# Room for the sixth head's output gates, and another order of loads and splits, in a decoder layer on one core

## The chip, the core and the metric

The kernel runs on one core of a Trainium2 chip. The core has five engines that work side by side, each through its own queue in order: TensorE (PE in the profile), VectorE (DVE), ScalarE (ACT), GpSimd (POOL) and SyncE (SP), which here issues most of the transfers (DMAs) between device memory and the core's memory (SBUF). Matmuls write to PSUM, a small memory of its own. The metric is device time in microseconds (us) for one launch; less is better.

## The reference, cut to what matters

One layer of a hybrid decoder: 1024 tokens of a prompt and 8 single tokens of samples, 1032 columns in all, 1024 channels, float32.

```python
h = _rmsnorm(x, lp['norm1_w']) * (1 + sc1) + sh1
qkv, gdn_gate, beta_raw, a_raw, sq, sk, sv, ga, gb = _split_in(h @ lp['w_in'])
...
def step(S, inp):
    u_n, w_n, a_n, qd_n, kd_n, last_n = inp
    v_new = u_n - jnp.einsum('bhck,bhkv->bhcv', w_n, S)
    o = jnp.einsum('bhck,bhkv->bhcv', qd_n, S) + jnp.einsum('bhij,bhjv->bhiv', a_n, v_new)
    S = S * last_n[..., None, None] + jnp.einsum('bhck,bhcv->bhkv', kd_n, v_new)
    return S, o
y_a = _gdn_out(o_a, gdn_gate, lp['gdn_onorm_w']) @ lp['w_gdn_out']
y_b = o_b @ lp['w_swa_out']
mix = (jax.nn.sigmoid(ga) * y_a + jax.nn.sigmoid(gb) * y_b) @ lp['w_o']
x = x + gt1 * mix
...
```

Here `step` runs over chunks of tokens, for 8 heads with a state S of 128 x 128 each; `_gdn_out` norms its output and multiplies with silu of the output gate; o_b is the output of a sliding-window attention with sinks. A gated FFN with a short convolution and a last norm follow. The samples use the same weights, but a recurrence of one step from a stored state (state_gdn_S), 512 KB for each head.

## The kernel before

Every large product is made three times in a rounded float format: a weight and an activation are each split into a high part (the rounded value, made by ScalarE, L129) and a low part (the rest, by VectorE, L130), and high x high, high x low and low x high are added in PSUM (`mm3`, L200 to L202). Columns come in three parts of 384, 384 and 264 (0, 1, 2; part 2 holds the samples). A weight column block of 128 is loaded by SP as `raw` (512 KB, L150) and split into `wh` and `wl`.

The stages are: conditioning, norm and attention (to about 400 us), the delta rule (to about 1116 us), the two branches' output projections (to about 1260 us), and then the output projection and the FFN.

In the delta stage a loop runs over heads 0 to 7. For each head h it weaves several streams into one order by priorities; the scheduler that lays out the engines' queues decides the rest. The streams are:

- `unit_inverse(h)`: the inverse of a triangular matrix for each of eight chunks of 128 tokens, by blocks of 16, 32 and 64. On PE its steps are L1065, L1071 (16 to 32), L1083, L1088 (32 to 64) and L1097, L1101 (64 to 128), each with copies by ScalarE and VectorE before the next; some blocks are rearranged by transfers (ud, MR, wd, T). The result is W.
- `delta_scan(h)`: a serial chain over eight chunks. For each chunk: L971 (K times the state S), y on VectorE (L972), L974 (W times y), s on ScalarE (L976), L978 (times kd), and the new S on VectorE (L990); L981 and L982 add the output o, which is later normed (osq, L996), transposed and multiplied with the head's output gates sg (L1010, in place), and stored to oa (L1015).
- `delta_prepare(h+1)`: transposes of K, Q and V of the next head (L210) and its products K K and K Q (L926, L927).
- fillers: the projections from w_in. For head h+2 the convolution inputs; the output gates of head h (`delta_gate`), 1032 columns into the tile sg, which exists once, so that the next head's gates are written only when the last ones are stored; the branch gates ga and gb, written to device memory (sga, sgb); and in the loop's last two rounds `early_out`.

`early_out` projects part 2 (and for two column blocks part 0) of the attention's output ob with w_swa_out, multiplies with gate tiles gt loaded from sgb, and stores to device memory. During scans 6 and 7 its products are paced (`spaced`): six matmuls for each link of the scan. Scan 7 also keeps its small operations (`self.small`), and the multiplications by gates are put behind the small operations that go before them (`passed`). At the seventh column block (i == 6) it issues the loads of six of the eight sample states.

`branches` finishes the projection of ob, computes the samples' one step (`sample_delta`: among its last operations are, for each head, a broadcast load of dlr, eight scalings on ScalarE, `scaled[h]`, an update of the state on VectorE and its store), and projects oa with w_gdn_out, in pairs of column blocks. `order(later, first)` makes the instructions of one list stand behind those of another in the queue of their engine, without a wait between engines. `issue_after` puts an instruction behind a given one in the order. Constants live in three pools: those of the whole run, and cp2, which stays open until after the branches.

Of the kernel before, what the change touches and what calls it, by code (L numbers as in the profile page):

```python
# [18 lines left out]
P = 128  # L19
NP = 1024  # L20
NS = 8
NT = NP + NS
KC = 8
H = 8
# [5 lines left out]
EARLY = (3, 4)  # L30
# [2 lines left out]
QUARTERS = [(0, 256), (256, 256), (512, 260), (772, 260)]  # L33
HALF = [(0, 512), (512, 520)]
QW = 260
KEPT = {"ident", "ones", "mhalf", "phalf", "vecs", "fcw", "mT", "a2"}
COL_GATE, COL_BETA, COL_SQ = 3072, 4096, 4112
COL_SK, COL_SV, COL_GA, COL_GB = 5136, 5392, 5648, 6672
# [26 lines left out]
class Step:  # L65
# [28 lines left out]
        return pool.tile(shape, dt, tag=tag, name=f"{tag}_{self.n}", **kw)  # L94

    def const(self, shape, name, dt=F32):
        pool = self.cp if name in KEPT else self.cp2
        return pool.tile(shape, dt, tag=name, name=name)


# [769 lines left out]
    def delta_gate(self, pa, pool, h):  # L870

        nc = self.nc
        sg = self.t(pool, [P, NT], "sg", bufs=1) if h + 1 < H else self.t(self.pz, [P, NT + 3], "z")[:, :NT]

        def gate_out(t, ps):
            lo, n = PARTS[t]
            th = self.t(pa, [P, 512], "th", bufs=2)[:, :n]
            nc.scalar.activation(th, ps, AF.Tanh, scale=0.5)
            nc.vector.scalar_tensor_tensor(sg[:, lo:lo + n], th, 1.0, ps, op0=ALU.add, op1=ALU.mult)

        self.project(self.win(COL_GATE + h * P), self.h, gate_out)
        nc.gpsimd.tensor_copy(self.sgs[:, h, :], sg[:, NP:NT])
        self.sg[h] = sg
        yield
# [263 lines left out]
    def sample_delta(self, pool2):  # L1148

        nc, I = self.nc, self.I  # L1150
# [18 lines left out]
        c, db = (self.flat_room(self.b1, "b1", x, 2) for x in "hl")  # L1169
# [50 lines left out]
        dlr = self.t(self.dr, [H, NS, P], "dlr")  # L1220
# [16 lines left out]
        for h in range(H):  # L1237
            if h % 4 == 0:
                yield
            d = db[:, h % 2 * NP:h % 2 * NP + NP].rearrange("p (b v) -> p b v", b=NS)  # L1240
            nc.sync.dma_start(d, dlr[h].unsqueeze(0).broadcast_to([P, NS, P]))
            for b in range(NS):
                made = nc.scalar.activation(d[:, b, :], d[:, b, :], AF.Copy, scale=kq[:, h, b, 0:1])
                self.scaled.setdefault(h, []).append(made)
                nc.vector.scalar_tensor_tensor(S0[h][:, b, :], S0[h][:, b, :], self.egb[:, b, 0, h:h + 1], d[:, b, :],
                                               op0=ALU.mult, op1=ALU.add)
            nc.gpsimd.dma_start(self.O[3][0][:, h].rearrange("b k v -> k b v"), S0[h])
# [84 lines left out]
    def early_out(self):  # L1332

        nc = self.nc
# [6 lines left out]
        for i, j in enumerate(EARLY_ORDER):  # L1341
            if i == 3:
                self.obX = {0: self.load_part(self.b1, self.ob, 0, "b1")}
                X.update(self.obX)
            now, w = w, load(EARLY_ORDER[i + 1]) if i < 7 else None
            if i == 6:
                with self.tc.issue_after(self.w_load.ins):
                    for h in range(6):
                        self.load_state(h, states[h // 3])
            for t in (2, 0) if j in EARLY else (2,):  # L1350
                lo, n = PARTS[t]
                s = self.t(self.gt[0], [P, 384], self.gt[1])[:, :n]
                nc.sync.dma_start(s, self.sgb[j][:, lo:lo + n])

                def out(t, ps):
                    with self.passed():
                        nc.vector.tensor_tensor(s, ps, s, op=ALU.mult)
                    nc.gpsimd.dma_start(self.ubd[t][j], s)

                for _ in self.project_steps(now, X, out, (t,), self.fill_psum):  # L1360
                    yield

    def branches(self, pool, pool2):
# [2 lines left out]
        ob = {**self.obX, 1: self.load_part(pool2, self.ob, 1)}  # L1366
        ub = [self.t(pool, [P, KC, n], f"t{t}", bufs=1) for t, (_, n) in enumerate(PARTS)]
        samples, rows, self.scaled = self.sample_delta(pool2), self.last_rows(), {}
        gate = lambda src, j, t: self.gate_part(pool if src is self.sga and j > 5 else self.gt[0], src[j][:, PARTS[t][0]:PARTS[t][0] + PARTS[t][1]], t)

        def yb_out(t, ps):
# [41 lines left out]
        for j0 in (0, 2, 4, 6):  # L1413
            w = []
            for j in (j0, j0 + 1):
                w.append(self.load_w(I["w_gdn_out"][0][:, j * P:(j + 1) * P]))
                for h in {1: range(3, H), 2: (6, 7)}.get(j, ()):
                    self.order(self.scaled[h], self.rounded)
            if 0 < j0 < 6:
                for j in (j0, j0 + 1):  # L1420
                    self.project(w[j - j0], oa, ya_out)
                continue
# [583 lines left out]

    def run(self):
        S, nc = ExitStack, self.nc
        self.constants()
        with S() as ca:  # L2010
            with S() as c:
                pool, psum = self.pool("p2", 1, ctx=c), self.pool("q2", 1, PSUM, ctx=c)
                for tag, bufs in dict(qst=8, raw=2, kh=2, kl=2, E=3, obt=2, pp=2, pc=2, o=2).items():
                    self.bufs[id(pool), tag] = bufs
# [112 lines left out]
```

## Time and profile before

| what | value |
|---|---|
| median of 3 runs (lowest, highest) | 2075.91 us (2066.82, 2076.16) |
| the profiled execution | 2069.76 us |
| its span | 2068.1 us |
| mean granted clock of PE | 0.990 |
| PE busy in 0 to 400 us | 375.15 us, mean clock 1.00 |
| PE busy in 400 to 1116 us | 698.20 us, mean clock 0.98 |
| PE busy in 1116 to 1260 us | 140.88 us, mean clock 0.99 |
| PE busy in 1260 to 2068 us | 795.00 us, mean clock 0.99 |

The last four rows are from the view that sums each engine's busy time in given stretches. The span is the time from the first to the last instruction of one execution. Granted clock is the share of the full TensorE clock that the chip's throttle gave. A row of a timeline has the start, the duration, the engine, the line, the operation, output and input, how often, and in brackets how long the engine stood idle before it and whom it waited for. The chain of waits goes back from the last instruction to what released it at each step.

### The profile page before, as it was taken

How to read it: one execution, taken by the hardware profiler on the slowest of the kernel's cores; microseconds unless marked ns; L12 is line 12 of the kernel's file. 1: busy time of each engine (PE TensorE's matmuls, PEld its weight loads, DVE VectorE, ACT ScalarE, POOL GpSimd, SP SyncE). 2: the span in 40 equal slices, each digit the busy share in tenths (PEclk: the TensorE clock that was granted, in tenths of full speed). 3: DMA queues.
4: the chain of work that ended last, by engine and by line, in shares of the span. 5: the costliest groups of instructions: out<-in, count | busy, mean ns of one | idle time of the engine just before them, and what ended most of it. 6: DMA issues, size and time to landing. Idle time of an engine off the chain costs nothing.

```text
span 2068.1 us, 41309 instructions
## 1 busy us (share of the span) xinstructions
PE 2009.2 (97%) x16245; PEld 1909.6 (92%) x16245; DVE 1356.6 (66%) x2714; ACT 901.7 (44%) x2233; POOL 525.0 (25%) x604
## 2 busy tenths in 40 slices
PE   7999998999999999989999999999999999999998
PEld 4987877799999999989989999999999999999998
DVE  5755767483655746646554575579876777679876
ACT  4664545443344343442442352345544444445444
POOL 2000000121321211201112010104556556543551
PEclk9999999999999999989999999999999999999999
DMA  9256443332322322312248774522333333377783
GB/s 303 62 145 211 137 168 117 100 98 63 83 82 57 78 70 52 92 37 61 64 144 243 233 242 115 174 67 89 98 98 100 111 93 93 124 277 279 265 281 129
DMA packets 300960, 275.75 MB, mean 133 GB/s; under 512 B 59731, under 2 KB 246832, under 8 KB 300749
## 3 DMA queue, kind: packets, MB, share of 16 engines
q1 hardware_dynamic: 294202, 250.66, 39.7%
q0 software_dynamic: 6064, 21.85, 3.0%
q8 instruction: 127, 2.08, 0.4%
q14 instruction: 69, 0.56, 0.1%
q10 hardware_dynamic: 498, 0.61, 0.1%
HBM read 212.93 MB, written 62.51 MB: 133 GB/s over the span
## 4 chain that ended last, share of the span: by engine, by line
PE 85%; DVE 6%; DMA 4%; ACT 3%; issue 1%; SPq 0%; POOL 0%; ACTq 0%; DVEq 0%; POOLq 0%
PE mm L200 19%; PE mm L201 18%; PE mm L202 18%; PE wv L200 3%; PE wv L202 3%; PE wv L201 3%; PE wy L202 2%; PE wy L200 2%; PE wy L201 2%; PE pv L672 1%; DMA raw<-in_w_swa_out_dram 1%; PE pt L210 1%; PE tp L210 1%; PE mm L284 1%; PE rc L978 1%
## 5 line engine op out<-in xcount | busy, mean ns | idle before, releaser
L200 PE MATMUL mm<-b1h,wh 128*128 128x384 f32 (+1 forms) x1520 | 498.1, 329 | 3.4 <-ACT gt L1322 1.6
L201 PE MATMUL mm<-b1l,wh 128*128 128x384 f32 (+1 forms) x1520 | 489.9, 323 | 0.0
L202 PE MATMUL mm<-b1h,wl 128*128 128x384 f32 (+1 forms) x1520 | 488.6, 324 | 0.0
L200 PEld LDWEIGHTS mm<-b1h,wh 128*128 128x128 f32 x1520 | 287.6, 189 | 12.0 <-issue 4.6
L201 PEld LDWEIGHTS mm<-b1l,wh 128*128 128x128 f32 x1520 | 287.6, 189 | 4.4 <-issue 3.1
L202 PEld LDWEIGHTS mm<-b1h,wl 128*128 128x128 f32 x1520 | 286.6, 189 | 3.7 <-issue 2.8
L130 DVE TENSOR_TENSOR wl<-raw,wh 128x1024 fp32r<-128x1024 f32 x82 | 102.6, 1252 | 65.9 <-ACT wh L129 63.7
L129 ACT ACTIVATE wh<-raw 128x1024 fp32r<-128x1024 f32 x83 | 87.1, 1049 | 131.1 <-PE mm L201 80.0
L201 PE MATMUL mm<-pk,w 128*128 128x260 f32 (+1 forms) x440 | 124.7, 284 | 1.1 <-DVE pk L130 1.1
L200 PE MATMUL mm<-pk,w 128*128 128x260 f32 (+1 forms) x440 | 124.7, 284 | 0.0
L202 PE MATMUL mm<-pk,w 128*128 128x260 f32 (+1 forms) x440 | 124.5, 283 | 0.0
L130 DVE TENSOR_TENSOR w<-ws,w 128x512 fp32r<-128x512 f32 x88 | 78.8, 896 | 38.9 <-ACT w L129 38.7
L1666 ACT COPY bml<-mm 128x256 f32<-128x256 f32 (+1 forms) x132 | 49.0, 371 | 102.0 <-PE mm L202 99.4
L200 PE MATMUL mm<-bmh,w 128*128 128x260 f32 (+1 forms) x320 | 90.3, 282 | 0.0
L202 PE MATMUL mm<-bmh,w 128*128 128x260 f32 (+1 forms) x320 | 90.2, 282 | 0.0
L200 PE MATMUL mm<-b2h,wh 128*128 128x384 f32 (+1 forms) x256 | 83.3, 327 | 2.6 <-ACT wh L129 2.6
L1721 DVE SCALAR_TENSOR_TENSOR fa<-fz,fcw,fa 128x512 f32<-128x512 f32 x88 | 73.3, 854 | 18.4 <-ACT fa L1719 18.1
L201 PEld LDWEIGHTS mm<-pk,w 128*128 128x128 f32 x440 | 83.2, 189 | 1.3 <-DVE pk L130 1.3
L201 PE MATMUL mm<-b2l,wh 128*128 128x384 f32 (+1 forms) x256 | 83.6, 327 | 0.0
L200 PEld LDWEIGHTS mm<-pk,w 128*128 128x128 f32 x440 | 83.2, 189 | 0.2 <-ACT bml L1666 0.2
L202 PEld LDWEIGHTS mm<-pk,w 128*128 128x128 f32 x440 | 83.4, 190 | 0.0
L202 PE MATMUL mm<-b2h,wl 128*128 128x384 f32 (+1 forms) x256 | 82.6, 325 | 0.0
(648 smaller groups left out, 5886.7 us busy)
## 6 DMA issues: line engine op xcount, KB each, us to landing
raw<-in_w_in_dram SPq DMA_DIRECT2D x59, 512.0 KB
ws<-in_w_ffn_down_dram SPq DMA_DIRECT2D x55, 256.0 KB
raw<-xd SPq DMA_DIRECT2D x47, 258.0 KB
raw<-in_w_ffn_down_dram SPq DMA_DIRECT2D x47, 256.0 KB
raw<-in_w_ffn_gate_dram SPq DMA_DIRECT2D x22, 512.0 KB
raw<-in_w_ffn_up_dram SPq DMA_DIRECT2D x22, 512.0 KB
qst<-in_w_mod_dram SPq DMA_DIRECT2D x16, 512.0 KB
raw<-in_w_mod_dram SPq DMA_DIRECT2D x16, 512.0 KB
```

Of the source, the lines that this page charges most:

```text
L129: return (self.nc.scalar.activation(hi, x, AF.Copy), (eng or self.nc.vector).tensor_tensor(lo, x, hi.bitcast(F32), op=ALU.subtract))
L130: (eng or self.nc.vector).tensor_tensor(lo, x, hi.bitcast(F32), op=ALU.subtract))
L200: mm(ps, whi, xhi, start=first, stop=False, **kw)
L201: mm(ps, whi, xlo, start=False, stop=False, **kw)
L202: self.last_mm = mm(ps, wlo, xhi, start=False, stop=last, **kw).ins
L210: self.nc.tensor.transpose(out, in_, self.ident[:p, :p])
L284: nc.tensor.matmul(ps[32 * j:32 * j + 32], self.cT[:, k0 + j, :], ws[j // 2][:, j % 2, :], start=k0 == 0, stop=k0 > 0)
L672: nc.tensor.matmul(pv[64 * r:64 * r + 64], V[:, n - back, ch], ps[:, r::2, :], start=back == 0, stop=back == (n > 0))
L978: yield step(nc.tensor.matmul(ds, kd[:, n, :], s, start=True, stop=True))
L1666: self.last_copy = nc.scalar.copy(r[p, i], x[p])
L1721: nc.vector.scalar_tensor_tensor(ai[:, c:e], zi[:, j + c:j + e], col(j), ai[:, c:e], op0=ALU.mult, op1=ALU.add)
```

## The change

It has five parts.

1. Ten constants that only the first stages read (SHORT; 4832 bytes of each partition) move from cp2 to a pool cp1 of the attention's context, which is closed after the attention.
2. A pool `side` of that size is opened then. It holds the output gates of head 5, the sixth (`sg5`). Heads 4 and 6 still share the one tile sg, but head 5's gates wait for neither.
3. In `early_out`, while a paced scan runs, the split of the next w_swa_out weight is ordered behind the last four of the scan's small operations that go before the place reached (only scan 7 keeps them).
4. The six states are loaded behind the last gate tile of the last column block (i == 7), no longer behind the weight at i == 6.
5. In `branches`, the scalings of heads 1 to 7 stand behind the split of the first w_gdn_out weight, those of heads 2 to 7 behind the second's (3 to 7 before), 6 and 7 behind the third's as before; and the broadcasts of dlr for heads 2 and 3 stand behind the load of the second weight, 4 and 5 behind the third's.

```diff
+SHORT = {"triu", "tril", "trilu", "stril", "sink", "qs", "kx", "vx", "zero", "a1"}
 KEPT = {"ident", "ones", "mhalf", "phalf", "vecs", "fcw", "mT", "a2"}
...
-        pool = self.cp if name in KEPT else self.cp2
+        pool = self.cp if name in KEPT else self.cp1 if name in SHORT else self.cp2
...
-        sg = self.t(pool, [P, NT], "sg", bufs=1) if h + 1 < H else self.t(self.pz, [P, NT + 3], "z")[:, :NT]
+        sg = self.sg5 if h == 5 else self.t(pool, [P, NT], "sg", bufs=1) if h + 1 < H else self.t(self.pz, [P, NT + 3], "z")[:, :NT]
...
-            nc.sync.dma_start(d, dlr[h].unsqueeze(0).broadcast_to([P, NS, P]))
+            self.spread[h] = nc.sync.dma_start(d, dlr[h].unsqueeze(0).broadcast_to([P, NS, P]))
...
-            if i == 6:
-                with self.tc.issue_after(self.w_load.ins):
-                    for h in range(6):
-                        self.load_state(h, states[h // 3])
-            for t in (2, 0) if j in EARLY else (2,):
+            if w and self.steps:
+                self.order(self.rounded, [x for n, x in self.small if n <= self.at // self.every + 1][-4:])
+            ts = (2, 0) if j in EARLY else (2,)
+            for t in ts:
                 lo, n = PARTS[t]
                 s = self.t(self.gt[0], [P, 384], self.gt[1])[:, :n]
-                nc.sync.dma_start(s, self.sgb[j][:, lo:lo + n])
+                gate = nc.sync.dma_start(s, self.sgb[j][:, lo:lo + n])
+                if i == 7 and t == ts[-1]:
+                    with self.tc.issue_after(gate.ins):
+                        for h in range(6):
+                            self.load_state(h, states[h // 3])
...
-                for h in {1: range(3, H), 2: (6, 7)}.get(j, ()):
+                for h in {0: range(1, H), 1: range(2, H), 2: (6, 7)}.get(j, ()):
                     self.order(self.scaled[h], self.rounded)
+                for h in {1: (2, 3), 2: (4, 5)}.get(j, ()):
+                    self.order([self.spread[h]], [self.w_load])
...
-        self.constants()
         with S() as ca:
             with S() as c:
+                self.cp1 = self.pool("cp1", 1, ctx=c)
+                self.constants()
...
             cg = S()
+            self.side = self.pool("side", 1, ctx=cg)
+            self.sg5 = self.t(self.side, [P, 1208], "sg")[:, :NT]
```

What it does to the queues shows at three places. The line numbers of the changed kernel are higher by one in the delta stage, so that L979 of it is L978 of the profile, and by up to seven in the branches. In the rows stand the line, the operation, output and inputs; mm is a projection, rc the scan's products, tp the inverse's and the transposes.

First TensorE's queue at the end of scan 4, from the last but one L978 on. Before:

```order
L978 MATMUL rc_9735<-s_9733,kd_8864 128x128
L982 MATMUL o_9698<-s_9733,A_8916 128x128
L202 MATMUL mm_10286<-b1h_12_150,wl_10255 128x384
L971 MATMUL rc_9742<-S_9739,K_7325 128x128
L981 MATMUL o_9698<-S_9739,Q_7326 128x128
L974 MATMUL rc_9745<-y_9741,W_4535 128x128
L978 MATMUL rc_9749<-s_9747,kd_8864 128x128
L982 MATMUL o_9698<-s_9747,A_8916 128x128
L1101 MATMUL tp_10183<-W_4535,UZ_9991 64x64 x8
L210 MATMUL tp_10876<-ident,K_9341 128x128 x4
```

In the changed kernel the same place of the queue, its rows 4718 to 4725, holds output projections of column part 2:

```order
L201 MATMUL mm_10321<-b1h_14_155,wh_10261 128x264
L202 MATMUL mm_10321<-b1l_15_156,wh_10261 128x264
L203 MATMUL mm_10321<-b1h_14_155,wl_10262 128x264
L201 MATMUL mm_10321<-b1h_14_155,wh_10261 128x264
L202 MATMUL mm_10321<-b1l_15_156,wh_10261 128x264
L203 MATMUL mm_10321<-b1h_14_155,wl_10262 128x264
L201 MATMUL mm_10321<-b1h_14_155,wh_10261 128x264
L202 MATMUL mm_10321<-b1l_15_156,wh_10261 128x264
```

The last links of scan 4, L1101 of inverse 5 and head 5's preparation moved apart: projections stand between them.

Second TensorE's queue at the end of scan 5. Before, from the same link of the chain on:

```order
L978 MATMUL rc_10723<-s_10721,kd_9872 128x128
L982 MATMUL o_10700<-s_10721,A_9924 128x128
L1071 MATMUL tp_11093<-T_11050,tmp_11091 32x32 x25
L971 MATMUL rc_10730<-S_10727,K_8333 128x128
L981 MATMUL o_10700<-S_10727,Q_8334 128x128
L1071 MATMUL tp_11093<-T_11050,tmp_11091 32x32 x7
L200 MATMUL mm_11201<-b1h_10_148,wh_11197 128x384
L201 MATMUL mm_11201<-b1l_11_149,wh_11197 128x384
```

After, rows 5239 to 5250 of the queue; three more links of the chain, L1102, eight transposes of K and four of vn follow them, up to scan 6's first L975 in row 5258:

```order
L979 MATMUL rc_10730<-s_10728,kd_9880 128x128
L983 MATMUL o_10707<-s_10728,A_9932 128x128
L1084 MATMUL tp_11140<-MR_11062,U_1744_10999 32x32 x16
L972 MATMUL rc_10737<-S_10734,K_8341 128x128
L982 MATMUL o_10707<-S_10734,Q_8342 128x128
L1089 MATMUL tp_11142<-T_11057,tmp_11141 32x32 x16
L975 MATMUL rc_10740<-y_10736,W_4543 128x128
L979 MATMUL rc_10744<-s_10742,kd_9880 128x128
L983 MATMUL o_10707<-s_10742,A_9932 128x128
L1098 MATMUL tp_11182<-MR_11062,UZ_11000 64x64 x8
L972 MATMUL rc_10751<-S_10748,K_8341 128x128
L982 MATMUL o_10707<-S_10748,Q_8342 128x128
```

No projection stands in these rows any more; inverse 6 has got further than before at the same link. The last steps of inverse 7 stand in a similar way: L1072, L1084, L1089, L1098 and L1102 follow each other (rows 5536 to 5540) directly ahead of scan 7's first L975, where they stood within scan 6 before.

Third the start of scan 7 in ScalarE's queue, where s is the scan's copy and wh the high half of a w_swa_out weight. Before:

```order
L129 ACTIVATE wh_12452<-raw_12450 128x1024
L129 ACTIVATE wh_12417<-raw_12415 128x1024
L976 ACTIVATE s_12263<-rc_12261,c_1909_11985 128x128
L976 ACTIVATE s_12276<-rc_12274,c_1909_11985 128x128
L129 ACTIVATE wh_12487<-raw_12485 128x1024
L976 ACTIVATE s_12290<-rc_12288,c_1909_11985 128x128
L129 ACTIVATE wh_12522<-raw_12520 128x1024
L976 ACTIVATE s_12304<-rc_12302,c_1909_11985 128x128
```

After:

```order
L977 ACTIVATE s_12270<-rc_12268,c_1909_11992 128x128
L130 ACTIVATE wh_12424<-raw_12422 128x1024
L977 ACTIVATE s_12283<-rc_12281,c_1909_11992 128x128
L130 ACTIVATE wh_12459<-raw_12457 128x1024
L977 ACTIVATE s_12297<-rc_12295,c_1909_11992 128x128
L130 ACTIVATE wh_12494<-raw_12492 128x1024
L977 ACTIVATE s_12311<-rc_12309,c_1909_11992 128x128
L997 ACTIVATE osq_1977_12319,so_12265<-o_12267 128x128 x4
L977 ACTIVATE s_12335<-rc_12333,c_1909_11992 128x128
```

Every split now has one s ahead of it. On SP's queue the states moved too: they stood between scan 7's fourth and fifth weight before, among gate tiles, and now stand behind the last gate tile and ahead of the next weight (raw_12812 of the branches):

```order
L151 DMA raw_12692<-in_w_swa_out_dram 128x8x128
L1353 DMA gt_12591<-sgb_2616 128x264
L151 DMA raw_12698<-in_w_swa_out_dram 128x8x128
L1353 DMA gt_12620<-sgb_2616 128x384
L1147 DMA b1h_1875_11810<-in_state_gdn_S_dram 128x8x128 x3
L1147 DMA b1l_1876_11811<-in_state_gdn_S_dram 128x8x128 x3
L151 DMA raw_12812<-in_w_swa_out_dram 128x8x128
L1147 DMA b1h_2051_12740<-in_state_gdn_S_dram 128x8x128 x2
L1437 DMA gt_12737<-sgb_2616 128x384
```

Behind the states stand one weight, two more states, a gate and the four loads of ob's part 1.

More of the change, by code (lines that the diff above doesn't have):

```diff
@@ L1368, in branches @@
         samples, rows, self.scaled = self.sample_delta(pool2), self.last_rows(), {}
+        self.spread = {}
         gate = lambda src, j, t: self.gate_part(pool if src is self.sga and j > 5 else self.gt[0], src[j][:, PARTS[t][0]:PARTS[t][0] + PARTS[t][1]], t)
```

## The prediction

> **What bounds the kernel now.** First the busy times of the page, then the waits of TensorE between 860 and 1210 us, which is where the change moves anything. The columns of the waits are total us, times, longest.
>
> ```profile
> PE 2009.2 (97%) x16245; PEld 1909.6 (92%) x16245; DVE 1356.6 (66%) x2714; ACT 901.7 (44%) x2233; POOL 525.0 (25%) x604
> PE rc L974 <- DVE y L972: 4.6, 4, 2.0
> PE rc L978 <- ACT s L976: 4.0, 3, 2.7
> PE mm L200 <- ACT wh L129: 2.6, 1, 2.6
> ```
>
> TensorE is busy for 2009.2 of 2068.1 us, and the change removes none of its work: its order holds the same products in another sequence. So the change can only win or lose idle time of PE, and time in which PE runs at a lower granted clock. Of the three largest waits, two are links of the scan's serial chain (L971, y, L974, s, L978, S, L971) and one is a weight that was split late. The next view is the busy time of each engine in chosen stretches; the first figure after the stretch is its length, then PE's busy time, and near the end stand the granted clock, the DMA share and GB/s.
>
> ```profile
> 915.00:930.00 15.00, 12.17 (x68) 10.15 (x67) 7.15 (x14) 11.83 (x49) 1.41 (x3) 0.66 0.11 41
> 1008.00:1018.00 10.00, 8.24 (x67) 7.00 (x66) 6.47 (x15) 8.15 (x39) 2.66 (x2) 1.00 0.32 107
> 1045.00:1063.00 18.00, 15.64 (x245) 13.49 (x244) 9.96 (x18) 7.37 (x15) 2.02 (x4) 1.00 0.54 145
> 1081.00:1117.00 36.00, 31.24 (x223) 30.65 (x222) 16.86 (x32) 10.25 (x24) 4.34 (x7) 0.91 0.80 230
> 1190.00:1200.00 10.00, 7.35 (x41) 7.03 (x41) 6.57 (x18) 6.80 (x15) 1.48 (x2) 0.83 1.07 380
> 1090.00:1100.00 10.00, 10.00 (x85) 9.94 (x84) 5.93 (x13) 4.66 (x14) 1.08 (x2) 1.00 1.14 319
> ```
>
> What a stretch loses is its length less PE's busy time, plus the length times what the clock lacks of 1. Scan 4's end (915 to 930): 2.83 + 15 x 0.34 = **7.9 us**. The start of head 6's preparation (1008 to 1018): **1.8**. Inverse 7 beside scan 6 (1045 to 1063): **2.4**. Scan 7 (1081 to 1117): 4.76 + 36 x 0.09 = **8.0**. The second weight of w_gdn_out (1190 to 1200): 2.65 + 1.7 = **4.35**. Together 24.5 us is all that the change can reach: 1.2% of the run.
>
> The 7.9 us in PE's own timeline (start, duration, line; in brackets the idle time before it):
>
> ```profile
> 914.75 0.39 PE L978 MATMUL rc<-s,kd 128*128 128x128 f32 x2
> 914.97 0.39 PE L982 MATMUL o<-s,A 128*128 128x128 f32 x2
> 917.03 0.49 PE L974 MATMUL rc<-y,W 128*128 128x128 f32 x2 [0.74 <-DVE y L972]
> 918.29 0.78 PE L978 MATMUL rc<-s,kd 128*128 128x128 f32 x2 [0.77 <-ACT s L976]
> 920.62 1.97 PE L1101 MATMUL tp<-W,UZ 64*64 64x64 f32 x16 [1.12 <-ACT W L1092]
> 925.52 0.63 PE L974 MATMUL rc<-vn,W 128*128 128x128 f32 x2
> ```
>
> No projection stands between these rows: each link of the chain is waited out, and from 918.29 on the matmuls take twice as long. From L978 at 914.75 to the last L978 of the scan are three links in 3.54 us, 1.18 each; from there to the next scan's first L974 it is 7.23 us.
>
> **The change, part by part.** The constants' new room costs nothing by itself: the same tiles are made by the same instructions, and PE's order is the old one up to scan 4's last links, at about 907 us. What it buys is a second place for the output gates of head 5, so that its projection need not wait until head 4's gates are stored.
>
> *The old voids.* In the new order scan 4's last links stand among projections, so the 7.9 us go. So do the 1.8 and the 2.4, since inverse 7's early steps and head 6's preparation get other neighbours: **-12.1**. What is late next is what those projections used to cover, one head later.
>
> *The end of scan 5* (20 rows of the new order, shown with the change). It is the same picture as scan 4's end, with six links of the chain instead of three and four steps of inverse 6 between them, and no projection. Six links at 1.18 and the tail of 7.23 are 14.3 us. The work in it: twelve scan matmuls at 0.22 (914.75 to 914.97), the inverse's steps L1083, L1088, L1097 and L1101 at 0.69, 0.69, 1.11 and 1.14 (next fence), and twelve transposes at about 0.11: 7.6 us. That is 6.7 lost, and some 1.5 after it until the clock is back, as behind 925.52. The least is links at the 0.95 us of an undisturbed scan,
>
> ```profile
> 1098.28 0.38 PE L971 MATMUL rc<-S,K 128*128 128x128 f32 x2
> 1099.23 0.38 PE L974 MATMUL rc<-y,W 128*128 128x128 f32 x2
> ```
>
> with the tail's 5 us of matmuls at full clock (2.2 less): 10.7 - 7.6 = 3. The most is all 4 us of work between the links at half clock as well: 12. I take **+8**, near scan 4's end, the nearest stretch.
>
> *Inverse 7.* Before, its steps stood inside scan 6, with projections between them. Now eight projections, then L1071, L1083, L1088, L1097 and L1101 stand one behind another ahead of scan 7's first L974. Each waits for copies of the one before. Rows in which such a pair stands apart (the last three are ScalarE's copies and L1101 itself):
>
> ```profile
> 1051.55 0.54 PE L1065 MATMUL tp<-MR,U 32*32 32x32 f32 x38
> 1055.03 0.37 PE L1071 MATMUL tp<-T,tmp 32*32 32x32 f32 x18
> ...
> 986.48 0.32 PE L1071 MATMUL tp<-T,tmp 32*32 32x32 f32 x14
> 988.52 0.69 PE L1083 MATMUL tp<-MR,U 32*32 32x32 f32 x32
> ...
> 1061.16 0.69 PE L1083 MATMUL tp<-MR,U 32*32 32x32 f32 x32 [0.47 <-DVE MR L1073]
> 1063.47 0.43 PE L1088 MATMUL tp<-T,tmp 32*32 32x32 f32 x14
> ...
> 907.67 0.69 PE L1088 MATMUL tp<-T,tmp 32*32 32x32 f32 x32
> 909.39 1.11 PE L1097 MATMUL tp<-MR,UZ 64*64 64x64 f32 x16
> ...
> 1071.04 0.58 ACT L1098 COPY UZ<-tp 64x512 f32<-64x512 f32 x1
> 1075.42 0.58 ACT L1102 COPY W<-tp 64x512 f32<-64x512 f32 x1
> 1073.97 1.14 PE L1101 MATMUL tp<-W,UZ 64*64 64x64 f32 x16
> ```
>
> From the end of one to the start of the next: 2.94, 1.72, 1.62, 1.03, then a copy of 0.58 on either side of L1101: 8.5 us. Of these the eight projections fill 1.0. So 7.5 us are idle, and the steps' own 4.5 us run partly at half clock: 7.5 to 11. Some of those gaps held other work in ScalarE's queue (splits of ob stand there around 1071), without which they may be shorter: 5 at the least. I take **+8**.
>
> *The end of scan 6.* ScalarE's new order has three splits of ob's last part ahead of a scan copy s. Their load is issued only once the head's previous product is through, and such a load took
>
> ```profile
> 1052.56 4.86 DMA b1l<-ob
> ```
>
> If other work covers it, nothing is lost; if the whole load shows, 4.9. Nearest is a load with half its time covered by the projections placed there: **+3**.
>
> *Scan 7.* Why it lost 8.0, by the chain of waits (start, us, what):
>
> ```profile
> 1077.78 6.03 DMA raw<-in_w_swa_out_dram
> 1083.91 1.06 ACT wh L129
> ...
> 1099.71 7.16 DMA gt<-sgb
> ...
> 1107.31 1.21 DVE wl L130
> 1108.53 0.66 DVE z L1010
> ```
>
> A split of w_swa_out stood in ScalarE's queue ahead of the scan's s and waited for its load; later VectorE waited for a gate tile whose load had been issued behind the states, and y waited behind that. The change orders each split behind the scan's small operations, and moves the states away, which answers both. But a weight still needs 6.0 + 1.1 + 1.2 = 8.3 us from issue to both halves, five weights pass in a scan of 27 to 35 us, 5.4 to 7 us each, and splits still stand ahead of scan copies in ScalarE's order (wh ahead of the next s after chunks 0, 1 and 2). With one load running ahead I expect three shortages of about 1.6 us, 4.8 in all: **-3.2** (0 to -8.0, either end being possible).
>
> *The states.* Six loads of 0.5 MB at 319 GB/s (1090 to 1100) are 9.9 us. Their issue held SP in two stretches, the longer being
>
> ```profile
> 1091.09 6.46 SPq L1146 DMA_DIRECT2D b1l<-in_state_gdn_S_dram x3
> ```
>
> Now they are issued behind scan 7's last gate and ahead of the next w_swa_out weight, two more states, a gate and part 1 of ob, which the branches' first products read. If 8 of the 9.9 us are hidden, **+1.5** or so remain; 0 if PE still has other work for so long, 4 if only 6 are hidden.
>
> *The branches.* The second w_gdn_out weight was late:
>
> ```profile
> 1186.10 7.59 DMA raw<-in_w_gdn_out_dram
> ...
> 1193.77 1.06 ACT wh L129
> ```
>
> Its load ran beside the broadcasts of dlr at 380 GB/s. With broadcasts 2 and 3 behind it, and the scalings of heads 1 to 7 behind the first rounding, it should take the 6 us of the row above at most and come earlier: **-4.0** (0 to -4.35). The scalings that move later end in stores that PE does not wait for.
>
> Sum: -12.1 + 8 + 8 + 3 - 3.2 + 1.5 - 4.0 = **+1.2 us**. Against the profiled execution of 2069.76 us that is 2071; the runs shown have a median of 2075.91, 6.15 above it, so the forecast is 2077.
>
> The least certain price is the clock. The gate let PE fall to half after idle times of 0.74 and 0.77 us (918.29), but here, after a longer one, it did not:
>
> ```profile
> 352.67 0.39 PE L634 MATMUL sc<-kh,qst 128*128 128x256 f32 x1 [2.35 <-DVE E L640]
> ```
>
> The Trainium skill, in TensorE: Matmul & The Clock Gate, section "Part 1: The HAM clock gate", says that the clock halves after about one idle window of some 3.4 us, that the window is free-running, and that it comes back after as long a busy time. By that rule none of the new gaps, all under 3 us, would cost any clock: an estimate from it leaves scan 5's end at 3 and inverse 7 at 7.5, and the sum at -4.3. The row of 918.29 speaks against the rule's length, the row of 352.67 for it, so I keep the half clock in my values.
>
> **The rivals.** *The voids close well (faster).* Links at 0.95 us and full clock at scan 5's end (3), short copies in inverse 7 (5), the load of ob hidden (0), scan 7 without a stall (-8.0), nothing for the states, -4.35 in the branches: -12.1 + 8 - 12.4 = -16.5, **2059**. For it: 1098.28 and 1099.23 show a scan running undisturbed as soon as no split stands in its way. Against it: it needs five separate ends at once, and half of it is 2068.
>
> *The states push the branches (slower).* Six states pass ahead of the weight and of ob's first part on one queue. If that weight is needed as soon as PE is through with scan 7, the 9.9 us show in full, and what follows on SP, the w_gdn_out weights too, moves along, so the 4 us there are not won: 1.2 - 1.5 + 9.9 + 4 = +13.6, **2089.5**. It decides from the point where PE has less than 8 us of other work ahead of that weight. For it: the DMA share of 1.14 in 1090 to 1100, no room beside the states. Against it: nothing waited for them before.
>
> *It doesn't do what it says.* Scan 7 stays paced by its loads, and the second w_gdn_out weight stays late: 1.2 + 3.2 + 4 = +8.4, **2084**. For it: 8.3 us a weight against 5.4 to 7.
>
> **How the numbers follow.** My forecast has a chance of 0.45, the faster rival 0.19, the slower 0.18, the third 0.18. 0.5% is 10.4 us, about what a measurement of this kernel can tell from no change; that is below 2065.5 or above 2086.3. The first case lies within it but for 0.04; of the faster one 0.13 lies below; of the slower one 0.14 above; of the third 0.04. So faster 0.15, same 0.64, slower 0.21. The range goes from 2063, between forecast and faster rival, to 2089, nearly the slower one's time.
>
> **What would show it.** After the change PE's stretch at scan 4's end should have no idle time over 0.3 us and clock 1.00; scan 5's end should have 3 to 5 us of idle time in waits of L974 and L978 and a clock near 0.6; inverse 7 waits at L1071, L1083, L1088 and L1097 of 1 to 3 us each; scan 7 splits that wait for raw, of 1 to 2 us; and L200's wait for wh near w_gdn_out should be gone. The forecast is wrong if the two new voids are covered by projections after all, or if a wait for raw of 8 us or more appears behind scan 7.

## The result, and the profile after

The changed kernel takes 2075.2 us (median of 15 runs, 2069.68 to 2080.51) against 2068.74 us of the kernel before (15 runs, 2065.11 to 2076.16): a ratio of 1.0030, 95% interval 1.0020 to 1.0039, or **6.2 us slower** (4.1 to 8.1). That is inside the 0.5% that the prediction called no change, and on its slower side. The forecast was 2077, 1.2 us above before. That it lies so near to 2075.2 is partly luck: the three runs known then had a median of 2075.91, and fifteen have one of 2068.74. The change itself was forecast 5 us too small.

The profiled execution took 2073.84 us with a span of 2071.9, 3.8 us longer than the one before. First the busy times, then PE's waits from 860 to 1230 us (total, times, longest), then the stretches that answer to those of before. Lines of the changed kernel are one higher in the delta stage, up to seven in the branches.

```profile
PE 2006.9 (97%) x16245; PEld 1908.9 (92%) x16245; DVE 1351.7 (65%) x2714; ACT 902.7 (44%) x2233; POOL 532.4 (26%) x604
```

```profile
PE mm L1174 <- DVE b2h L1166: 5.5, 1, 5.5
PE rc L975 <- DVE y L973: 3.2, 4, 1.6
PE rc L979 <- ACT s L977: 2.8, 5, 1.1
PE tp L1084 <- DVE MR L1074: 2.0, 1, 2.0
...
PE mm L203 <- DVE wl L131: 1.5, 1, 1.5
```

```profile
890.00:1007.00 117.00, 115.28 (x1091) 112.01 (x1079) 70.45 (x139) 42.11 (x115) 17.63 (x24) 0.99 0.21 56
1007.00:1026.00 19.00, 15.04 (x112) 13.22 (x106) 5.41 (x13) 11.94 (x51) 1.49 (x3) 0.82 0.18 60
1038.00:1062.00 24.00, 20.62 (x144) 19.47 (x144) 17.25 (x55) 10.94 (x29) 5.37 (x9) 1.00 0.60 170
1070.00:1088.00 18.00, 12.63 (x254) 11.41 (x253) 3.27 (x7) 6.17 (x14) 0.54 (x1) 0.72 0.29 89
1088.00:1122.00 34.00, 33.43 (x247) 32.80 (x246) 16.74 (x35) 10.36 (x28) 7.03 (x11) 1.00 0.71 205
1122.00:1142.00 20.00, 13.41 (x67) 12.17 (x65) 7.72 (x15) 3.74 (x5) 3.44 (x5) 0.83 0.89 283
1210.00:1225.00 15.00, 13.28 (x74) 12.74 (x73) 11.20 (x34) 9.02 (x28) 2.65 (x3) 1.00 0.87 287
```

Row by row: scan 4's end is dense now (115.28 of 117 us, clock 0.99). Scan 5's end, scan 6's end and inverse 7 idle 4.0, 3.4 and 5.4 us, the first and the last at clocks of 0.82 and 0.72. The rest of scan 7 (1088 to 1122) is dense at full clock: its two stalls are gone. New is the start of the branches (1122 to 1142): 6.6 us idle and a clock of 0.83, where the kernel before had one gap of 0.5. The last row is the second w_gdn_out weight, 1.7 us idle at full clock. At scan 5's end only 1.2 of the 4.0 us are waits of the chain's L975 and L979; 1.6 stand ahead of L1102, the inverse's last step, and 1.2 ahead of the transposes behind it.

The new wait is the largest of all, 5.5 us at L1174, a product of the samples' step. By the queue it is a small operation of VectorE (b2h, L1166) that came late, since it stood behind the multiplication by a gate tile that had not landed (L1377). First the rows of SyncE's queue (SPq) ahead of it, then the chain of waits, then VectorE's rows and PE's:

```profile
1110.14 2.52 SPq L1147 DMA_DIRECT2D b1h<-in_state_gdn_S_dram  x3
1112.71 5.88 SPq L1147 DMA_DIRECT2D b1l<-in_state_gdn_S_dram  x3
```

```profile
1122.64 1.01 SPq L1147
1123.70 2.21 SPq L1147
1126.00 2.10 SPq L1437
1128.15 6.58 DMA b2l<-ob
1134.76 0.85 ACT b2h L130
```

```profile
1133.82 0.56 DVE L1377 TENSOR_TENSOR t<-mm,gt 128x384 f32<-128x384 f32 x1 [8.15 <-DMA gt<-sgb]
1134.30 0.28 DVE L1166 TENSOR_TENSOR b2h<-b2h 128x128 f32<-128x128 f32 x1
```

```profile
1134.63 0.59 PE L1174 MATMUL mm<-ones,b2h 128*128 128x1 f32 x2 [5.50 <-DVE b2h L1166]
```

The six states went out from 1110 to 1118.6, then a weight and two more states; the gate tile (L1437) was issued at 1126.00 and ob's part 1 at 1128.15, just before PE ran out of other work. The chain runs through ob, not through the gate tile: PE's product at 1135.65 needs ob's split, so two late loads end here almost together. In the kernel before the states were through at 1097.6, and its first gate tile was issued at 1116.64.

Three marks that all kernels have cut the traces into stages: scan 4's first L974, scan 7's first L974, scan 7's last L978, and the first matmul on bmh and pk that waits in the output projection (1285.59 us before).

| stage | before | after | difference |
|---|---|---|---|
| A: start of scan 4 to start of scan 7 | 241.0 | 242.3 | +1.3 |
| B: scan 7 | 34.5 | 28.8 | -5.7 |
| C: end of scan 7 to the output projection | 169.7 | 176.9 | +7.2 |

The three add up to +2.8, and the spans differ by 3.8, where the medians differ by 6.2 by their ratio: the profiled execution before lay 1.0 us above its median, the one after 1.4 below.

### The profile page after: what moved, and what is told of

Same layout as the page of the kernel before. It is cut to its first block, busy times and chain, and to the rows that moved or that the text cites. A ratio compares the mean times of both kernels' runs of the same rounds, so it can differ in the third digit from the quotient of the medians.

```text
span 2071.9 us, 41313 instructions
## 1 busy us (share of the span) xinstructions
PE 2006.9 (97%) x16245; PEld 1908.9 (92%) x16245; DVE 1351.7 (65%) x2714; ACT 902.7 (44%) x2233; POOL 532.4 (26%) x604
## 4 chain that ended last, share of the span: by engine, by line
PE 84%; DMA 6%; DVE 5%; ACT 3%; issue 1%; SPq 1%; POOL 0%; DVEq 0%; POOLq 0%; ACTq 0%
PE mm L201 18%; PE mm L202 18%; PE mm L203 18%; PE wv L203 3%; PE wv L201 3%; PE wv L202 3%; PE wy L203 2%; PE wy L201 2%; PE wy L202 2%; PE pv L673 1%; PE tp L211 1%; DMA raw<-in_w_swa_out_dram 1%; PE pt L211 1%; PE mm L285 1%; DMA qst<-in_w_mod_dram 1%
## 5 line engine op out<-in xcount | busy, mean ns | idle before, releaser
L201 PE MATMUL mm<-b1h,wh 128*128 128x384 f32 (+1 forms) x1520 | 496.8, 328 | 3.2 <-ACT gt L1323 1.6
L201 PEld LDWEIGHTS mm<-b1h,wh 128*128 128x128 f32 x1520 | 287.1, 189 | 11.4 <-issue 4.6
L201 PE MATMUL mm<-pk,w 128*128 128x260 f32 (+1 forms) x440 | 124.6, 283 | 0.0
L201 PE MATMUL mm<-bmh,w 128*128 128x260 f32 (+1 forms) x320 | 90.3, 282 | 0.0
L201 PE MATMUL mm<-b2h,wh 128*128 128x384 f32 (+1 forms) x256 | 83.2, 328 | 0.7 <-ACT b2h L130 0.4
L201 PEld LDWEIGHTS mm<-pk,w 128*128 128x128 f32 x440 | 83.1, 189 | 0.2 <-ACT bml L1673 0.2
```

The lines of the kernel that those rows point to most:

```text
L201: mm(ps, whi, xhi, start=first, stop=False, **kw)
```

## The experiments

Two theories to begin with: **A**, the moved states hold up the branches; **B**, the voids that the room moved cost more than those that it fills. From the first four runs came **C**, below. Every kernel is the changed one with parts undone or altered, so the parts are named by their numbers: 1 and 2 the room, 3 the splits behind the scan's small operations, 4 the states behind the last gate, 5 the branches. Part 1, the constants' pool, stays in all twelve; where the room is said to be undone, only part 2 is. The twelve were timed in five rounds beside the kernel before. A difference in us is the ratio less 1, times 2069 us; stages are from one profiled execution each.

| kernel | parts | ratio, 95% interval | us | A | B | C |
|---|---|---|---|---|---|---|
| changed | 1 2 3 4 5 | 1.0030 (1.0020 to 1.0039) | +6.2 | 242.3 | 28.8 | 176.9 |
| e1_states_back | 1 2 3 5 | 1.0028 (1.0014 to 1.0041) | +5.8 | 240.8 | 38.0 | 167.0 |
| e2_no_room | 1 3 4 5 | 1.0018 (1.0003 to 1.0032) | +3.7 | 238.4 | 28.8 | 178.4 |
| e3_room_only | 1 2 | 0.9999 (0.9982 to 1.0015) | -0.2 | 244.6 | 29.1 | 168.9 |
| e4_splits_branches | 1 3 5 | 1.0002 (0.9990 to 1.0014) | +0.4 | 237.5 | 37.0 | 168.9 |
| e5_room_branches | 1 2 5 | 1.0000 (0.9986 to 1.0013) | 0.0 | 242.4 | 28.7 | 167.3 |
| e6_states_gpsimd | all, states on GpSimd | 1.0026 (1.0011 to 1.0042) | +5.4 | 249.7 | 28.8 | 167.6 |
| e7_states_after_ob | all, states behind ob | 0.9997 (0.9987 to 1.0007) | -0.6 | 240.1 | 30.0 | 170.0 |
| e8_no_splits | 1 2 4 5 | 1.0034 (1.0023 to 1.0046) | +7.0 | 244.3 | 29.7 | 177.7 |
| e9_inverse_first | 1 2 5, inverse 7 first | 0.9988 (0.9976 to 0.9999) | -2.5 | 243.7 | 31.3 | 169.2 |
| e10_inverse_first_ob | as e9, states behind ob | 1.0007 (0.9992 to 1.0021) | +1.4 | 245.1 | 29.3 | 175.5 |
| e11_states_only | 1 4 | 1.0014 (1.0002 to 1.0026) | +2.9 | 239.1 | 31.6 | 176.4 |
| e12_gate_first | all, one gate ahead of the states | 1.0051 (1.0037 to 1.0065) | +10.6 | 242.2 | 29.4 | 184.2 |

**e1: the states back.**

```diff
+            if i == 6:
+                with self.tc.issue_after(self.w_load.ins):
+                    for h in range(6):
+                        self.load_state(h, states[h // 3])
...
-                if i == 7 and t == ts[-1]:
-                    with self.tc.issue_after(gate.ins):
-                        for h in range(6):
-                            self.load_state(h, states[h // 3])
```

> The changed kernel with its fourth part alone undone: the six states are issued behind the weight at i == 6 again. Theory A (the moved states block SyncE's queue at the start of the branches, so that the first gate tile comes late and PE waits 5.5 us at L1174 and then runs at half clock for 6.8 us, 9 us in all): that wait is gone, a wait of the scan's y or s of 1 to 3 us comes back in scan 7, and the time is 5 to 9 us below the changed kernel, within 3 us of the kernel before. Theory B (the loss is the room: the voids at the ends of scans 5 and 6 and in inverse 7): the time stays 5 to 7 us above the kernel before.

The wait at L1174 went, as theory A said, and stage C fell by 9.9 us. But the time stayed at +5.8, as theory B said. Neither had it right: scan 7 grew to 38.0 us, with another wait than that of before. SyncE's rows, then a piece of the chain of waits, then PE's wait:

```profile
1084.47 0.38 SPq L151 DMA_DIRECT2D raw<-in_w_swa_out_dram  x1
1084.95 0.53 SPq L1147 DMA_DIRECT2D b1h<-in_state_gdn_S_dram  x1
...
1088.99 6.91 SPq L1147 DMA_DIRECT2D b1l<-in_state_gdn_S_dram  x3
1096.01 1.95 SPq L151 DMA_DIRECT2D raw<-in_w_swa_out_dram  x1
```

```profile
1096.01 7.83 DMA raw<-in_w_swa_out_dram
...
1103.86 1.06 ACT wh L130
```

```profile
PE mm L201 <- ACT wh L130: 2.7, 1, 2.7
```

A split that is ordered late frees its raw tile late; the loads of the next weights then stand behind the states, and the product waits for its weight. The scan's own waits are 1.0 us at most now; it is the projection that waits for a split. The stages of this execution, at 2069.76 us one of the fastest of its twelve, add up to only 0.6 us above before; what holds e1 at +5.8 shows in the comparison with e5, below.

**e2: the room undone** (head 5's gates in the shared tile).

```diff
-        sg = self.sg5 if h == 5 else self.t(pool, [P, NT], "sg", bufs=1) if h + 1 < H else ...
+        sg = self.t(pool, [P, NT], "sg", bufs=1) if h + 1 < H else ...
```

> The changed kernel with its second part alone undone: head 5's output gates use the one shared tile again (the constants' pool still closes after the attention). Theory A: scan 4's void of 8 us is back and those at scans 5, 6 and inverse 7 are gone; delta stage 2 us shorter than in the changed kernel; the wait at L1174 of about 5 us stays, so 3 to 5 us above the kernel before. Theory B: the loss is gone, within 1.5 us of the kernel before or below it.

Theory A's number came out: +3.7, L1174 waits 6.3 us, stage A 3.9 us shorter than in the changed kernel.

**e3: the room alone**, and **e4: splits and branches alone.** e3 takes parts 3, 4 and 5 out, e4 parts 2 and 4.

> The kernel before with parts one and two alone (constants' pool and the room for head 5's gates). Theory A: the voids at scan 5's end (about 7 us), scan 6's end (3) and in inverse 7 (about 9) stand against scan 4's void and two smaller ones (12): 1 to 4 us above the kernel before; scan 7 loses 8 us as before. Theory B: 5 to 8 us above the kernel before.

> The kernel before with parts three and five alone (splits behind the scan's small operations; scalings and broadcasts of the branches). Both theories: the 2.7 us wait of s for the split in scan 7 is gone (with its clock 3 to 4 us), the wait for the second w_gdn_out weight falls from 2.65 to about 1.5 us without half clock (2 to 3 us); the y wait behind the gate tile (2 us and clock 1.7) stays: 4 to 7 us below the kernel before. If the split's order only moves the stall to the next weight, 0 to 2 us below.

e3's expectations failed on scan 7, and of e4's the second came out (+0.4, the stall moved). With the room alone scan 7 does not stall at all (29.1 us; the largest wait behind its first product is the row below), although splits and states are where they were in the order:

```profile
PE rc L979 <- ACT s L977: 0.2, 1, 0.2
```

```profile
1080.06 2.18 SPq L1147 DMA_DIRECT2D b1h<-in_state_gdn_S_dram  x3
1082.28 5.25 SPq L1147 DMA_DIRECT2D b1l<-in_state_gdn_S_dram  x3
```

Its scan 7 begins at 1086.85. The room has put inverse 7 without projections ahead of the scan, four weights were issued before 1077, and the states load in that void. With the splits alone (e4) scan 7 has the same late weight as in e1 (L201 waits 2.6 us for wh) and takes 37.0 us.

So **theory C**: the room costs 3.4 us in stage A (242.4 on average in the seven kernels that have it and leave inverse 7's order alone apart from e6, against 239.0 in the four that don't) and gets 5.4 us back in scan 7 (29.1 for 34.5) without any of the other parts. Moving the states then has nothing left to win there and only takes them to the branches.

**e5: room and branches**, **e8: no splits.** e5 leaves out parts 3 and 4, e8 part 3 alone.

> The changed kernel without its parts three and four: the room for head 5's gates and the new order of the branches, splits and states as before. Theory C (the room alone already lets the states load during inverse 7's void, so scan 7 runs without a stall; moving the states then only takes them to the branches): no wait over 0.5 us in scan 7, no wait at L1174, the wait for the second w_gdn_out weight falls from 2.5 to about 1.4 us and without half clock: 2 to 4 us below the kernel before. If the splits or the moved states are needed for scan 7: 0 to 3 us above it.

> The changed kernel without its third part (splits behind the scan's small operations). Theory C: scan 7 has no wait over 0.6 us even so, since its loads come in time with the states out of the way; L1174 still waits 5 to 6 us: within 2 us of the changed kernel. If the splits' order is what cleared scan 7: waits of s or y of 1 to 3 us come back, 2 to 5 us above the changed kernel.

Theory C holds in both on the waits: scan 7 takes 28.7 and 29.7 us without the splits' order, so with the room there that order gains nothing. The two differ by part 4 alone: L1174 waits 4.0 us in e8 and not in e5, stage C is 177.7 and 167.3, the time +7.0 and 0.0. e1 and e5 differ by part 3 alone: scan 7 takes 38.0 and 28.7 us, the time is +5.8 and 0.0. So with the states in their old place the splits' order costs all that the room won there, and with the states moved it changes nothing that can be told (+7.0 in e8, +6.2 with it). The gain of 2 to 4 us that e5 was to show isn't there: it is below what the runs can tell (interval -2.9 to +2.7 us), though the wait for the second w_gdn_out weight is 1.1 us in place of e3's 2.5.

**e6: the states on GpSimd's queue.**

```diff
-        self.nc.sync.dma_start(self.S0[h], self.I["state_gdn_S"][0][:, h].rearrange("b k v -> k b v"))
+        (queue or self.nc.sync).dma_start(self.S0[h], self.I["state_gdn_S"][0][:, h].rearrange("b k v -> k b v"))
...
-                            self.load_state(h, states[h // 3])
+                            self.load_state(h, states[h // 3], nc.gpsimd)
```

> The changed kernel with the six state loads issued on GpSimd's queue in place of SyncE's. If SyncE's blocked queue holds up the gate tile and ob's part 1: the 5.5 us wait at L1174 falls under 2 us, half clock there is gone, and the time is 4 to 8 us below the changed kernel. If the 16 engines' bandwidth is what they lack: the gate tile lands as late, the wait stays over 4 us, and the time is within 2 us of the changed kernel.

It doesn't settle queue against bandwidth for the branches: `issue_after` orders within one engine, and on another queue the states were issued some 50 us earlier, beside the round trips of inverse 7, which then waited longest of all. Stage C got 9.3 us shorter (167.6), and stage A 7.4 us longer (249.7):

```profile
1058.81 2.92 POOL L1147 DMA_DIRECT2D b1l<-in_state_gdn_S_dram  x3 [5.48 <-PE mm L203]
1061.72 2.63 POOL L1147 DMA_DIRECT2D b1h<-in_state_gdn_S_dram  x3
```

```profile
PE tp L1066 <- DVE MR L1062: 8.9, 1, 8.9
```

It does show that a free queue is not enough. SyncE issued the round trip's small loads (T, 32 KB each) without delay, but the last took 13.49 us beside the states, where it took 2.68 us in the changed kernel. From 1062 to 1076 the DMA engines' busy share was 1.07, against 0.63 in the changed kernel. The chain of waits of e6, then of the changed kernel:

```profile
1062.48 13.49 DMA T<-wd
```

```profile
1065.25 2.68 DMA T<-wd
```

**e7: the states behind ob's part 1.**

```diff
-                if i == 7 and t == ts[-1]:
-                    with self.tc.issue_after(gate.ins):
-                        for h in range(6):
-                            self.load_state(h, states[h // 3])
...
         ob = {**self.obX, 1: self.load_part(pool2, self.ob, 1)}
+        with self.tc.issue_after(self.part_load.ins):
+            for h in range(6):
+                self.load_state(h, self.states[h // 3])
```

> The changed kernel with the six state loads behind ob's part 1 and the first two gate tiles of the branches on SyncE's queue. Theory C, queue or bandwidth: the wait at L1174 falls under 1.5 us; the later gate tiles and the samples' products L1200 may wait instead, up to 3 us: 3 to 8 us below the changed kernel. If the wait only moves to the next gate tile: within 2 us of the changed kernel.

SyncE's rows:

```profile
1118.87 0.32 SPq L1436 DMA_DIRECT2D gt<-sgb  x1
...
1128.01 2.00 SPq L1279 DMA_DIRECT2D b2l<-ob  x4
1130.05 6.35 SPq L1147 DMA_DIRECT2D b1h<-in_state_gdn_S_dram  x3
```

The gate tile goes out at 1118.87 in place of 1126.00 us, although scan 7 began 3.6 us later in this execution, L1174 does not wait, and the whole loss is gone: -0.6 us against before, 6.8 less than the changed kernel. Everything else of the change is in it. It moves the states out of the way of the queue and of the transfers at once, so which of the two delayed the gate tile and ob more stays open.

**e11: part 4 alone**, on the kernel before, and **e12: only the gate tile moved ahead.** e12 issues the states behind the branches' first gate tile (and the weight ahead of it).

> The kernel before with part four alone (the states behind scan 7's last gate tile). If the place of the states alone makes the loss: L1174 waits 4 to 6 us for VectorE and PE runs at half clock there for 7 to 10 us (7 to 10 us in all), while in scan 7 the y wait of 2.0 us and its clock of 1.7 us go and the s wait of 2.7 us stays: 3 to 7 us above the kernel before. If the place costs only together with the room: within 2 us of it.

> The changed kernel with only the branches' first gate tile and one w_swa_out weight moved ahead of the six states; ob's part 1 stays behind them. If the one gate tile that VectorE waited for was the cause: L1174 does not wait, nothing else waits over 1 us in its place, 5 to 8 us below the changed kernel. If the states keep everything behind them late: L1174's wait is gone, but the next product waits 3 to 6 us for ob's part 1 (its split b2h or its load), with half clock behind it: within 2.5 us of the changed kernel, 4 to 8 us above the kernel before.

PE's waits in e11, then in e12, then SyncE's rows in e12:

```profile
PE mm L1174 <- DVE b2h L1166: 4.0, 1, 4.0
PE rc L979 <- ACT s L977: 2.8, 2, 2.6
```

```profile
PE mm L201 <- ACT b2h L130: 9.5, 1, 9.5
```

```profile
1115.19 0.32 SPq L1437 DMA_DIRECT2D gt<-sgb  x1
1115.61 4.87 SPq L1147 DMA_DIRECT2D b1h<-in_state_gdn_S_dram  x3
1120.52 8.17 SPq L1147 DMA_DIRECT2D b1l<-in_state_gdn_S_dram  x3
1128.79 4.79 SPq L1147 DMA_DIRECT2D b1h<-in_state_gdn_S_dram  x2
...
1135.40 1.98 SPq L1279 DMA_DIRECT2D b2l<-ob  x4
```

e11 costs 2.9 us, at the edge of what the first theory said: stage C +6.7, scan 7 -2.9, since without the room there is a stall of the scan's y to win. e12 shows that the gate tile was only the first in the row: with it out of the way L1174 does not wait, and PE waits 9.5 us for ob's part 1, issued at 1135.40 behind eight states that held SyncE for 17.8 us. The second expectation had the place and not the size (3 to 6 us): the states start 5.5 us later than in the changed kernel (1115.61 for 1110.14) and ob 7.3 us later (1135.40 for 1128.15), and the kernel is 4.4 us slower than that one.

**e9 and e10: a better version?** Inverse 7's L1084 waited 3.5 us in e5, since VectorE's part of it stood behind a split whose weight was still loading. Both order the splits of the next weights behind inverse 7's small operations (in e10 with e7's place for the states).

```diff
             now, w = w, load(EARLY_ORDER[i + 1]) if i < 7 else None
+            if w:
+                self.order(self.rounded, self.inverse)
...
```

> The room and the branches' order (as in e5), and the splits of the two w_swa_out weights that scan 7 needs ordered behind inverse 7's small operations. In e5 L1084 of inverse 7 waited 3.5 us for VectorE, which stood behind a split whose weight was still on its way. If that wait ends with the split out of its way: L1084 waits 1.7 us or less, 1.5 to 3 us below e5, 2 to 4 us below the kernel before. If the splits then come late for scan 7: a wait for wh of 1 to 3 us there and no gain over e5.

> As e9, with the states behind ob's part 1 (as in e7). Scan 7 shares its loads with nothing, so its waits are under 0.5 us each, and L1174 does not wait: within 1.5 us of e9, 2 to 4 us below the kernel before. If the room's voids (7, 3 and 8 us) are the floor: no different from e5 and e7.

e9 is the only one of the twelve whose interval lies below the kernel before: 2.5 us less (0.2 to 5.0), by so little that among twelve it may be chance. Its profile doesn't say why: L1084 waits 2.5 us, no longer 3.5, but scan 7 takes 31.3 us, 2.6 more than in e5. So whether and where it gains stays open, and the expectation that e10 would come out like it failed (+1.4, interval -1.7 to +4.3). In e10 L1174 does not wait, but its profiled execution, the slowest of its twelve, lost time later in stage C: from 1215 to 1235 us PE was idle for 2.3 us, in waits for w_gdn_out weights, at a clock of 0.83.

## Why the prediction was right and wrong

- **What bounds the kernel** held: PE does the same work, and the difference is idle time and clock, for the most part in the stages named: 2.8 of the spans' 3.8 us. Another 1.9 stand ahead of scan 4, where the clock fell in the attention (see the last section).
- **The old voids** (-12.1) went, and what was late next was what the text named, with these losses by its own formula: scan 5's end 4.0 + 19 x 0.18 = 7.4 (forecast 8), inverse 7 5.4 + 18 x 0.28 = 10.4 (forecast 8, range 5 to 11), scan 6's end 3.4 (forecast 3). At scan 5's end most of the idle time stood at L1102 and the transposes, and not in waits of L974 and L978 as the text said. PE's rows of inverse 7 show the picture that was forecast, each step waiting for the copies of the one before:

```profile
1075.42 0.69 PE L1084 MATMUL tp<-MR,U 32*32 32x32 f32 x32 [2.04 <-DVE MR L1074]
1076.95 1.42 PE L1089 MATMUL tp<-T,tmp 32*32 32x32 f32 x32 [0.84 <-ACT tmp L1086]
1079.39 1.94 PE L1098 MATMUL tp<-MR,UZ 64*64 64x64 f32 x16 [1.01 <-DVE MR L1095]
1082.00 1.96 PE L1102 MATMUL tp<-W,UZ 64*64 64x64 f32 x16 [0.67 <-ACT UZ L1099]
1084.63 0.80 PE L975 MATMUL rc<-vn,W 128*128 128x128 f32 x2 [0.67 <-ACT W L1103]
```

- **The formula** was not exact. Idle time at half clock counts in it twice, once as idle and once as lacking clock. By it stage A would have grown by 9.1 us (7.4 + 10.4 + 3.4 - 12.1); between the marks it grew by 1.3, and by 3.4 between the averages with and without the room. Counting twice is not shown to be all of it: over the whole stage PE's idle time went from 10.3 to 15.4 us at a mean clock of 0.96 both times, and its busy time fell from 230.7 to 226.9 us for the same work. So the room's net cost, forecast at +6.9, was some 3.5 us too high.
- **Scan 7** (-3.2) was under-sized: -5.7. The step that failed is "three shortages of about 1.6 us": the largest wait inside the scan is now 0.3 us. The forecast took the loads' rate as the limit and overlooked that the void ahead of the scan, forecast in the same text, is time in which loads run: the room alone brings 5.4 us of it (e3).
- **The states** (+1.5, at most 4) is the term that failed: "If 8 of the 9.9 us are hidden". Stage C shows 7 to 10 us (before to e11 6.7, e1 to the changed kernel 9.9, e5 to e8 10.4). Little or nothing was hidden. The forecast names the gate and ob's part 1 among what stands behind the states, but its rival sets the cover against the weight alone, and both leave out the samples' small operations behind the gate in VectorE's queue. What PE waited for was not the weight: L1174 waited 5.5 us behind the gate tile, and ob's part 1 landed 0.1 us after that wait had ended (1134.73). The slower rival had the place and the price (9.9) right. It was wrong in what follows: the second w_gdn_out weight came early enough to leave 1.7 us of idle time all the same.
- **The branches** (-4.0): 1.7 us idle at full clock in place of 4.35, so -2.6. As a change of its own it can't be told from nothing (e3 to e5).
- **The third rival** (the parts don't do what they say) was right for part 3 alone: with the states in their old place the late split moves the stall from the scan to the projection (e1, e4).
- **The range** held the time; the chance of "within 0.5%" was the right one to put first. That the sign of the change came out right is luck too: the forecast was above before because of the room's voids, and with the room and the branches alone the time is 0.0 (e5); the measured loss is the states', which it put at 1.5. 1.2 was a sum in which errors of both signs met (room 3.5 us too high, scan 7 2.5 too high, the branches 1.4 too low, states some 5 to 9 too low).

## What to carry to other kernels

A large transfer that is not urgent is best placed by what stands behind it on its queue, not by what it stood ahead of: list the transfers behind it, who reads each, and how much other work that engine has until then. A void on the bounding engine is not only lost time: loads run in it, so a stall behind it can vanish without any further edit; measure each part of a change with and without the others. Here part 4 shortens scan 7 only where the room is not or the splits are ordered late, and part 3 lengthens it unless the states are moved. Order a split behind an urgent operation only if the buffer that it frees has time to spare.

## What the runs showed of the chip

In these traces PE's half clock lasts for multiples of some 3.4 us, the run's end apart. The records of the granted clock below full speed, from 1000 to 1100 us, as start, length and clock:

```
changed         1016.0  6.8 0.50    1077.4 10.2 0.50
e3_room_only    1008.8 13.7 0.50    1077.0 13.7 0.50
e5_room_branches 1012.2  6.8 0.50   1073.6 13.7 0.50
```

Scan 5's end has the same kind of gaps in all three (0.2 to 1.6 us each), yet is at half clock for 6.8 us or 13.7 us. The plainest case is the gap of 2.35 us in the attention that the prediction sets against the half clock. It is the same in all fourteen profiled executions (2.34 to 2.36 us): nine stayed at full clock there, and in five the clock fell to half for 3.4 to 10.2 us (the changed kernel from 353.8 for 6.8 us). Such steps are as large as several of the differences sought here, so stages of single executions are told apart by a few us at best. The Trainium skill, in TensorE: Matmul & The Clock Gate, section "Part 1: The HAM clock gate", gives a free-running window of some 3.4 us; the lengths agree with that, while its idle time of a whole window before the clock falls does not: no gap at scan 5's end is longer than 1.6 us, and PE was at half clock there all the same.

The issue of a load can hold its queue for several us: three states held SyncE for 2.2 us in one row and for 8.2 us in another (e3 at 1080.06, e12 at 1120.52), and a load on a free queue can still be late beside another queue's (e6, 13.49 us for T).
